# First MLP of a decoder trunk: down products with the features on the partitions, summed in place on the residual

## Chip, core and metric

The kernel runs on one NeuronCore of a Trainium2 chip. The metric is device time in microseconds (us) from the first to the last instruction of the program, with what the device does around it; the median of several executions is given. In what follows PE is TensorE (matrix products, into PSUM), ScalarE is ACT in the profile, VectorE is DVE, GpSimd is POOL, and SP is the engine whose queue issues most DMAs.

## What is computed

The reference is a trunk of two layers over 512 tokens with 1024 features, all in float32:

```
for i in range(2):
    x = x + mixer_i(rms_norm(x, norm_mix[i]))        # 0: latent attention, 1: gated linear attention
    x = x + square(relu(rms_norm(x, norm_mlp[i]) @ w_up[i])) @ w_down[i]   # 1024 -> 4096 -> 1024
return rms_norm(x, final_norm)
```

This case is about the first of the two MLPs, that of layer 0. Behind it comes the norm of layer 1's gated linear attention, which wants its input with the features on the partitions. Behind the second MLP comes the final norm and the output, which is written with the tokens on the partitions.

## The kernel before

**Products in three parts.** Each float32 operand is split into a high part, rounded to the fast float32 format (`fp32r`), and the low rest. A product is high.high + high.low + low.high: three matmuls into one PSUM bank. `split` (lines 110 and 113) makes the two parts, the high one on ScalarE, the low one on VectorE; `piece` does it for a block of weights and puts the parts in the rooms `wh` and `wl`, four of each. A room has 1152 elements a partition and holds 1024; `at` says at which element the weights begin: `W_AT` is 128, `AT_UP` is 124 for the high and 60 for the low part. The normed input of the MLP lies at an offset of its own (`X_AT`, 44), and the tile `T` with its quadrant combinations begins at element 4 of its room. Hidden activations and their parts lie in "slots" (`slot("B")`), 512 elements each, from the slot's start; four pairs of slots are the rooms of the hidden parts (`parts_room`), used in turn.

**The MLP in blocks and quadrants.** The hidden width of 4096 is worked off in eight blocks of 512. The first block's up product is done plainly (`up_first`), the last block's down product too, at the end; the seven steps between do the down product of one block and the up product of the next. Each of the two is cut into quadrants (token halves, halves of the feature and hidden range) and done with seven quadrant products in place of eight, after the scheme of Strassen and Winograd, with sums and differences of quadrants on VectorE and in the weight loads (GpSimd's DMAs that add). `step` is the order of the first of the seven steps, in which up and down products alternate; `step_in_halves` is that of the other six, first the up products, then the down products. `quadrants()` makes the combinations of the input.

**Up and down products.** `up_product` (matmuls at line 962) has the weights as the stationary operand and the input as the moving one: output with hidden features on the partitions, 24 matmuls of 128x256. `down_product` (matmuls at line 971) has the hidden parts as the stationary operand and the weights as the moving one: output with the tokens on the partitions, two token tiles of 512 features each, 12 matmuls of 128x512. A PSUM tile of two banks (`d`, `e`) or two single banks (`u`) takes it.

**The sums.** The seven down products of a step are added up in five sums of 128x1024: S11, S12, S21, SU and S5. Four lie in the room of the residual `xall` (its eight tiles `xT[0..7]` have the features on the partitions), S5 in a tile of its own. A sum is carried on either by copying it into PSUM first, letting the product add to it and copying it back (`onto`, ScalarE), or by a VectorE addition. In the second MLP (`nxt` is None) `residual()` turns the residual into token-major form on PE (line 910), so that the sums start from it. In the first MLP (`nxt` is the next norm) the sums start from nothing (`opening` in `step`): the first copies overwrite `xall`, and the residual is saved before in DRAM as `x_kept` by a DMA on SP's queue (line 1166, after the load of d12) and loaded again at the end, in four pieces, into the `comb` tiles of four weight quadrants that are no longer used (`before_next`, line 1184, `kept`).

**The end of the first MLP.** Per output feature tile (`p`, eight of them in two groups of four): four transposes on PE turn the sums' 128x128 pieces into the PSUM bank (line 1233), 12 matmuls of 128x512 add the last block's plain down product (line 1240), VectorE adds the kept residual and writes `xT[m]` (line 1242), and `nxt.add` scales, splits and squares it for the next norm (lines 262, 263, 248 to 252). The hidden parts of the last block lie in the four rooms of `parts_room`. The next norm's mean comes from a product at line 277.

**What sets the order.** Every engine runs its own instructions in the order the program has them for that engine; the framework that builds the kernel places instructions by a plan of its own with costs, so that it may put a later line ahead of an earlier one where the data allow it. DMAs are issued on SP's and GpSimd's queues in order. Waits between engines are semaphores.

Of the kernel before, what the change touches and what calls it, by code (L numbers as in the profile page):

```python
# [50 lines left out]
def trunk_kernel(ctx: ExitStack, tc: tile.TileContext, t_in: dict, out: bass.AP):  # L51
# [763 lines left out]
    def mlp(layer, nrm, nxt=None):  # L815
# [7 lines left out]
        if nxt:  # L823
            dram = es.enter_context(tc.tile_pool(name=f"spill{layer}", bufs=1, space=bass.MemoryType.DRAM))
            x_kept = dram.tile([P, ND, S], F32, name="x_kept")

# [3 lines left out]
        sums = [xall[:, 2 * i : 2 * i + 2].rearrange("p a t -> p (a t)") for i in range(4)]  # L830
        sums.append(fast.tile([P, 2 * S], F32, tag="sum", name="sum5"))
        S11, S12, SU, S21, S5 = sums
# [70 lines left out]
        def residual():  # L903
            def turned(tag, c, th):
# [59 lines left out]
        def down_product(t, a, parts, start):  # L964
            wh, wl = piece(a, 2, 512)
# [8 lines left out]
        def step(b, q, r, after):  # L974
            opening = nxt is not None
# [7 lines left out]
            def add(total, t):  # L983
                if opening:
                    ACT.activation(total, t, AF.Copy)
                else:
                    DVE.tensor_tensor(total, t, total, ALU.add)

            def onto(tag, total, a, parts, fresh=False):
                t = two_banks(tag)  # L990
                if not fresh:
                    ACT.activation(t, total, AF.Copy)
                down_product(t, a, parts, fresh)
                ACT.activation(total, t, AF.Copy)
# [12 lines left out]
            if opening:  # L1007
                ACT.activation(S11, d, AF.Copy)
            e = two_banks("e") if opening else begun(d)
# [5 lines left out]
            down_product(e, d12, parts_of_quad(q21), opening)  # L1015
            DVE.tensor_tensor(S11, e, S11, ALU.add)
# [58 lines left out]
            def down_21():  # L1075
                onto("d", S21, d22, parts_of_quad(q21, -1.0), opening)
                after("d22")
# [9 lines left out]
        def step_in_halves(b, q, r, after):  # L1087
# [9 lines left out]
            def onto(total, a, parts):  # L1097
                pair = [bank("u"), bank("u")]
                cols = [total[:, i * 512 : (i + 1) * 512] for i in range(2)]
                for p, c in zip(pair, cols):  # L1100
                    copied(p, c)
                down_product(pair, a, parts, False)
                for p, c in zip(pair, cols):
                    copied(c, p)
# [38 lines left out]
            DVE.tensor_tensor(S11, e, S11, ALU.add)  # L1143
# [9 lines left out]
            DVE.tensor_tensor(S12, e, S12, ALU.add)  # L1153
            after("d12")
            down_product(d, ds3, parts_of_quad(q12), False)
            DVE.tensor_tensor(SU, d, SU, ALU.add)
# [4 lines left out]
        if not nxt:  # L1161
            residual()
        for name in ("S1", "dS1", "d11", "A1", "d12", "dS3", "A2", "d22"):
            if name == "dS3" and nxt:
                with tc.issue_after(queued.ins):
                    SP.dma_start(x_kept, xall)
            queued = fetch(0, name)
        last_raw, last, gain, kept = [], [[], []], [], []
# [12 lines left out]
        def before_next(name):  # L1181
            if name in ("d11", "S1", "d12", "dS3"):
                t = by_k(comb(home[name]), 2)
                SP.dma_start(t, x_kept[:, 2 * len(kept) : 2 * len(kept) + 2])
                kept.append(t)
# [30 lines left out]
        if nxt:  # L1216
            room = [parts_room[(turn[0] + k) % 4] for k in range(4)]
# [5 lines left out]
            for c in range(2):  # L1223
# [5 lines left out]
                for j, p in enumerate(ps_):  # L1229
                    for t in range(NT):  # L1230
                        o = t % 2 * 512 + j * P
                        src = (S11, S12, S21, SU)[2 * c + t // 2][:, o : o + P]
                        PE.matmul(p[:, t * P : (t + 1) * P], src, ident, start=t == 0, stop=False, is_transpose=True, skip_group_check=True)
                for j, p in enumerate(ps_):
                    if j % 2 == 0:
                        w = piece(last_raw[c][:, :, j * P : (j + 2) * P], 4, 256)
                    for k in range(4):
                        wh, wl = cut(w, slice(None), k, slice(j % 2 * P, (j % 2 + 1) * P))
                        for n, (a, x) in enumerate(((wh, room[k][0]), (wh, room[k][1]), (wl, room[k][0]))):
                            PE.matmul(p, a, x, start=False, stop=k == 3 and n == 2, skip_group_check=True)  # L1240
                    m = 4 * c + j
                    DVE.tensor_tensor(xT[m], p, kept[m // 2][:, m % 2], ALU.add)
# [615 lines left out]
```

## Time and profile before

| | |
|---|---|
| median of 3 executions | 1046.12 us (1045.90 to 1046.43) |
| profiled execution, span from its first to its last instruction | 1044.9 us |
| PE busy | 1035.0 us, 99% |
| weight loads of PE busy | 903.9 us, 87% |
| VectorE busy | 876.9 us, 84% |
| ScalarE busy | 696.8 us, 67% |
| first MLP, first up product of the steps to the last down product | 206.79 to 474.67 us |
| its last products | to 500.13 us |
| second MLP, residual transposes to the last down product | 743.23 to 1014.64 us |
| read from HBM, written | 144.49 MB, 4.19 MB |

How to read it: the profiled execution's own time is the span; the timed executions, which have no profiler, lie some 1.2 us above it. "Busy" of PE includes the latency of the last matmul of each run, so 99% doesn't mean that every cycle does work; the rate of a run of matmuls is read from the pieces of the chain of waits, which give the start of a piece, its length, and how many instructions it has. In a row of the groups view stand the line, engine, operation, output and inputs, shape, count, then the busy time and the mean duration of one; behind the second bar the idle time of the engine just before and who ended it. In a row of the timeline stand start, length, engine, line; idle time before the instruction and its releaser stand in brackets.

### The profile page before, as it was taken

What the parts mean: (1) busy time and instruction counts of PE and PEld (TensorE: products, weight loads), DVE (VectorE), ACT (ScalarE), POOL (GpSimd) and SP (SyncE); (2) the same over time, 40 slices, a digit from 0 to 9 for tenths busy, and PEclk for the clock granted to TensorE, in tenths of its full rate; (3) what the DMA queues carried; (4) which work ended last, traced back from release to release, by engine and by line L of the source; (5) the groups of instructions that cost most, each with busy time, mean ns of one, the idle gap of its engine ahead of it and who ended that gap; (6) DMA issues with size and microseconds to landing.
All of it is one profiled execution on the core that took longest, in us unless ns stands there. A gap on an engine that the chain in (4) does not pass through costs nothing.

```text
span 1044.9 us, 15747 instructions
## 1 busy us (share of the span) xinstructions
PE 1035.0 (99%) x5966; PEld 903.9 (87%) x5966; DVE 876.9 (84%) x1340; ACT 696.8 (67%) x1122; POOL 114.3 (11%) x128
## 2 busy tenths in 40 slices
PE   9999999999999999999999999999999999999997
PEld 8788888899899899898888888888889989989986
DVE  7889977988989989989687399469798999898993
ACT  8667754577776776785445566555677677677784
POOL 8400010301101101000000000000011111110000
PEclk9999999999999999999999999999999999999999
DMA  7401235769878778644212222165488778778422
GB/s 232 122 21 41 81 95 147 224 166 215 216 191 202 178 203 202 161 136 126 77 55 82 87 74 75 48 162 147 95 241 201 185 202 198 194 191 191 111 81 81
DMA packets 120717, 149.98 MB, mean 144 GB/s; under 512 B 9568, under 2 KB 86368, under 8 KB 120512
## 3 DMA queue, kind: packets, MB, share of 16 engines
q1 hardware_dynamic: 96144, 117.76, 35.4%
q0 software_dynamic: 22400, 29.36, 18.0%
q10 hardware_dynamic: 2096, 1.84, 0.6%
q8 instruction: 47, 0.77, 0.3%
q14 instruction: 30, 0.25, 0.1%
HBM read 144.49 MB, written 4.19 MB: 142 GB/s over the span
## 4 chain that ended last, share of the span: by engine, by line
PE 94%; DVE 3%; ACT 2%; issue 0%; DMA 0%; ACTq 0%; SPq 0%; DVEq 0%
PE ps L971 25%; PE ps L962 25%; PE ps L118 10%; PE ps L120 10%; PE ps L119 10%; PE ps L1279 2%; PE ps L1240 2%; PE ps L1499 1%; PE ps L135 1%; PE ps L421 1%; PE ps L1626 1%; DVE wl L113 1%; PE ps L1766 0%; PE ps L1549 0%; PE ps L684 0%
## 5 line engine op out<-in xcount | busy, mean ns | idle before, releaser
L971 PE MATMUL ps<-wh,set 128*128 128x512 f32 x784 | 245.7, 390 | 0.3 <-ACT set L110 0.3
L110 ACT ACTIVATE wh<-wraw 128x1024 fp32r<-128x1024 f32 x139 | 146.4, 1056 | 110.2 <-PE ps L119 42.6
L113 DVE TENSOR_TENSOR wl<-wraw,wh 128x1024 fp32r<-128x1024 f32 x139 | 169.7, 1222 | 39.0 <-ACT wh L110 38.7
L971 PEld LDWEIGHTS ps<-wh,set 128*128 128x128 f32 x784 | 147.0, 188 | 30.7 <-ACT set L110 0.7
L962 PE MATMUL ps<-T,wh 128*128 128x256 f32 x896 | 154.9, 275 | 0.0
L971 PE MATMUL ps<-wl,set 128*128 128x512 f32 x392 | 152.6, 389 | 0.0
L113 DVE TENSOR_TENSOR wl<-comb,wh 128x1024 fp32r<-128x1024 f32 x112 | 136.8, 1221 | 18.5 <-ACT wh L110 18.3
L110 ACT ACTIVATE wh<-comb 128x1024 fp32r<-128x1024 f32 x112 | 118.3, 1057 | 47.6 <-issue 28.7
L962 PEld LDWEIGHTS ps<-T,wh 128*128 128x128 f32 x896 | 135.4, 188 | 0.4
L962 PE MATMUL ps<-T,wl 128*128 128x256 f32 x448 | 123.4, 275 | 0.0
L962 PE MATMUL ps<-set,wh 128*128 128x256 f32 x672 | 117.1, 276 | 0.0
L118 PE MATMUL ps<-set,wh 128*128 128x512 f32 x280 | 109.7, 392 | 0.0
L119 PE MATMUL ps<-set,wh 128*128 128x512 f32 x280 | 109.6, 392 | 0.0
L120 PE MATMUL ps<-set,wl 128*128 128x512 f32 x280 | 109.3, 391 | 0.0
L962 PEld LDWEIGHTS ps<-set,wh 128*128 128x128 f32 x672 | 102.6, 188 | 1.3
L962 PE MATMUL ps<-set,wl 128*128 128x256 f32 x336 | 92.7, 276 | 0.0
L971 PEld LDWEIGHTS ps<-wl,set 128*128 128x128 f32 x392 | 73.6, 188 | 14.7
L962 PEld LDWEIGHTS ps<-T,wl 128*128 128x128 f32 x448 | 84.1, 188 | 0.1
L962 PEld LDWEIGHTS ps<-set,wl 128*128 128x128 f32 x336 | 63.1, 188 | 0.0
L120 PEld LDWEIGHTS ps<-set,wl 128*128 128x128 f32 x280 | 52.6, 188 | 11.1
L119 PEld LDWEIGHTS ps<-set,wh 128*128 128x128 f32 x280 | 52.6, 188 | 11.1 <-DVE set L750 0.2
L118 PEld LDWEIGHTS ps<-set,wh 128*128 128x128 f32 x280 | 52.6, 188 | 10.7
(415 smaller groups left out, 2015.4 us busy)
## 6 DMA issues: line engine op xcount, KB each, us to landing
comb<-in_mlp_w_down_dram SPq DMA_DIRECT2D x74, 512.0 KB, 4.1
wraw<-in_mlp_w_up_dram SPq DMA_DIRECT2D x18, 1024.0 KB, 5.6
comb<-in_mlp_w_down_dram POOLq DMA_DIRECT2D x28, 512.0 KB, 6.5
wraw<-in_mlp_w_up_dram SPq DMA_DIRECT2D x28, 512.0 KB, 5.6
wraw<-in_gla_w_in_dram SPq DMA_DIRECT2D x12, 1024.0 KB, 5.2
comb<-in_mlp_w_up_dram SPq DMA_DIRECT2D x14, 512.0 KB, 4.4
comb<-in_mlp_w_up_dram POOLq DMA_DIRECT2D x14, 512.0 KB, 6.4
wraw<-in_mlp_w_up_dram POOLq DMA_DIRECT2D x14, 512.0 KB, 7.6
```

What stands on the lines that cost most here:

```text
L110: order(ACT.activation(hi, src, AF.Copy))
L113: lo_eng.tensor_tensor(lo, src, f(hi), ALU.subtract)
L118: PE.matmul(psum, wh, xh, start=start, stop=False)
L119: PE.matmul(psum, wh, xl, start=False, stop=False)
L120: PE.matmul(psum, wl, xh, start=False, stop=stop)
L135: PE.transpose(psum, src, ident[: src.shape[0], : src.shape[0]])
L421: PE.matmul(p, w[:, i, j * P : (j + 1) * P], x, start=start, stop=stop)
L962: PE.matmul(o, a_, x_, start=start and j == 0 and k == 0 and n == 0, stop=k == KH - 1 and n == 2, skip_group_check=True)
L971: PE.matmul(o, x_, w_, start=start and k == 0 and n == 0, stop=k == 1 and n == 2, skip_group_check=True)
L1240: PE.matmul(p, a, x, start=False, stop=k == 3 and n == 2, skip_group_check=True)
L1279: PE.matmul(o, a, b_, start=False, stop=k == 3 and n == 2, skip_group_check=True)
L1499: PE.matmul(p[:, t - t0], k[:, t * P : (t + 1) * P], moving[:, t], start=True, stop=True)
```

## The change

All of it is in the first MLP; the second one keeps its form. Five things:

1. `down_product` takes the weights as the stationary operand and the hidden parts as the moving one: four feature tiles of 128x256, 24 matmuls. The weights' parts are put at `AT_UP` in their rooms.
2. The sums S11, S12, S21 and SU are the quadrants of the residual itself: feature half by token half of `xall`, as strided views of 4 x 256. `laid` gives PSUM tiles the same form. `residual()` does for the first MLP what the scheme needs of start values: SU is negated, and S21 becomes -S21 - SU.
3. `opening` is gone: the first step adds to its sums as the second MLP's does (`begun`, `add` on VectorE, `onto` with a copy first).
4. `x_kept`, its DMA to DRAM and the four loads of `kept` are gone.
5. At the end there are no transposes: the first matmul of each final product opens its bank, and VectorE adds `xT[m]` in place. The last of the four rooms of hidden parts is no longer the oldest of `parts_room` but a `comb` tile, the one that S1's weights had.

```diff
-            x_kept = dram.tile([P, ND, S], F32, name="x_kept")
...
+        if nxt:
+            S11, S12, S21, SU = (xall[:, c * KH : (c + 1) * KH, t] for c in range(2) for t in (first, second))
+        else:
+            S11, S12, SU, S21 = (xall[:, 2 * i : 2 * i + 2].rearrange("p a t -> p (a t)") for i in range(4))
...
         def residual():
+            if nxt:
+                ACT.activation(SU, SU, AF.Copy, scale=-1.0)
+                DVE.scalar_tensor_tensor(S21, S21, -1.0, SU, ALU.mult, ALU.subtract)
+                return
...
         def down_product(t, a, parts, start):
-            wh, wl = piece(a, 2, 512)
+            wh, wl = piece(a, 2, 512, at=AT_UP if nxt else (W_AT, W_AT))
+            if nxt:
+                for j in range(4):
+                    o = t[j // 2][:, j % 2 * TH : (j % 2 + 1) * TH] if isinstance(t, list) else t[:, j * TH : (j + 1) * TH]
+                    for k in range(2):
+                        xh, xl = cut(parts, slice(None), slice(k * TH, (k + 1) * TH))
+                        a_h, a_l = (w_[:, k, j * P : (j + 1) * P] for w_ in (wh, wl))
+                        for n, (w_, x_) in enumerate(((a_h, xh), (a_h, xl), (a_l, xh))):
+                            PE.matmul(o, w_, x_, start=start and j % 2 == 0 and k == 0 and n == 0, stop=k == 1 and n == 2, skip_group_check=True)
+                return
...
-            if opening:
-                ACT.activation(S11, d, AF.Copy)
-            e = two_banks("e") if opening else begun(d)
+            e = begun(d)
...
-                onto("d", S21, d22, parts_of_quad(q21, -1.0), opening)
+                onto("d", S21, d22, parts_of_quad(q21, -1.0))
...
-            if name == "dS3" and nxt:
-                with tc.issue_after(queued.ins):
-                    SP.dma_start(x_kept, xall)
...
-            if name in ("d11", "S1", "d12", "dS3"):
-                t = by_k(comb(home[name]), 2)
-                SP.dma_start(t, x_kept[:, 2 * len(kept) : 2 * len(kept) + 2])
-                kept.append(t)
...
-            room = [parts_room[(turn[0] + k) % 4] for k in range(4)]
+            spare = fast.tile([P, 2 * S], F32R, tag=f"comb{home['S1']}", bufs=1, name=uname("comb"))
+            room = [parts_room[(turn[0] + k) % 4] for k in range(3)] + [(spare[:, :S], spare[:, S:])]
...
-                    for t in range(NT):
-                        o = t % 2 * 512 + j * P
-                        src = (S11, S12, S21, SU)[2 * c + t // 2][:, o : o + P]
-                        PE.matmul(p[:, t * P : (t + 1) * P], src, ident, start=t == 0, stop=False, is_transpose=True, skip_group_check=True)
-                for j, p in enumerate(ps_):
...
-                            PE.matmul(p, a, x, start=False, stop=k == 3 and n == 2, skip_group_check=True)
+                            PE.matmul(p, a, x, start=k == 0 and n == 0, stop=k == 3 and n == 2)
                     m = 4 * c + j
-                    DVE.tensor_tensor(xT[m], p, kept[m // 2][:, m % 2], ALU.add)
+                    DVE.tensor_tensor(xT[m], p, xT[m], ALU.add)
```

44 lines of the change are left out of this document (20 added, 24 removed).

## The prediction

> **What bounds the kernel now.** I read the page first, then the chain of waits around the first MLP, then the engines' busy time in that stretch.
>
> ```profile
> span 1044.9 us, 15747 instructions
> ...
> PE 1035.0 (99%) x5966; PEld 903.9 (87%) x5966; DVE 876.9 (84%) x1340; ACT 696.8 (67%) x1122; POOL 114.3 (11%) x128
> ...
> PE 94%; DVE 3%; ACT 2%; issue 0%; DMA 0%; ACTq 0%; SPq 0%; DVEq 0%
> PE ps L971 25%; PE ps L962 25%; PE ps L118 10%; PE ps L120 10%; PE ps L119 10%; PE ps L1279 2%; PE ps L1240 2%; PE ps L1499 1%; PE ps L135 1%; PE ps L421 1%; PE ps L1626 1%; DVE wl L113 1%; PE ps L1766 0%; PE ps L1549 0%; PE ps L684 0%
> ```
>
> TensorE (PE) is the bound: 94% of the chain that ended last is its matmuls, half of that the up products (L962) and down products (L971). So what the change does to the time is read from PE's stream. The two MLPs, each from its first product (or residual transpose) to its last down product, stand in the windows view; the columns after the stretch are its length and each engine's busy us, then granted clock, DMA share and GB/s.
>
> ```profile
> 206.79:474.67 267.88, 267.73 (x1765) 244.17 (x1764) 240.84 (x266) 200.00 (x278) 31.93 (x27) 1.00 0.74 183
> 743.23:1014.64 271.41, 271.23 (x1796) 247.58 (x1795) 245.04 (x270) 202.64 (x280) 29.88 (x24) 1.00 0.70 174
> ```
>
> In the first MLP's 267.88 us PE idles 0.15 us, at the full clock. VectorE (240.84 us) and ScalarE (200.00 us) have room, DMA too. A saving on PE is therefore a saving in time, and every nanosecond added per matmul is a loss: nothing covers it.
>
> **The transposes removed.** Pieces of the chain of waits at the end of the first MLP (start, length, what):
>
> ```profile
> 474.83 1.75 PE ps L1233 x16
> 476.58 10.91 PE ps L1240 x48
> 487.49 1.75 PE ps L1233 x16
> 489.23 10.90 PE ps L1240 x48
> ```
>
> The 32 transposes that turn the token-major sums stand on the chain with nothing idle before or behind them, 2 x 1.75 = 3.50 us. Gone from PE: -3.50 us. The 96 products behind them stay, now opened by their own first matmul.
>
> **The down products.** A product was 12 matmuls of 512 columns (hidden parts stationary, weights moving); it becomes 24 of 256 (weights stationary, hidden parts moving). The window of the first MLP has 392 + 196 = 588 of the old ones, so 49 products, and 1176 matmuls after.
>
> ```profile
> L971 PE MATMUL ps<-wh,set 128*128 128x512 f32 x392 | 122.9, 390 | 0.2 <-ACT set L110 0.2
> ...
> L971 PE MATMUL ps<-wl,set 128*128 128x512 f32 x196 | 76.3, 389 | 0.0
> ```
>
> The 390 ns is latency, pipelined; the rate is in the chain:
>
> ```profile
> 206.95 2.74 PE ps L962 x24
> ...
> 766.84 2.75 PE ps L971 x12
> ...
> 588.45 1.42 PE ps L1626 x12
> ...
> 596.39 2.48 PE ps L1626 x21
> ```
>
> An up product, already 24 matmuls of 256 columns with weights stationary, takes 2.74 us; a down product of 12 by 512 takes 2.75. At the up product's rate (114 ns a matmul) the new form costs the same: 49 x (2.74 - 2.75) = -0.5 us, which is rounding; I take 0. But the third and fourth rows are matmuls of the same 128x256 shape in the linear-attention stage, and they come at 1.42/12 = 118 ns and 2.48/21 = 118 ns. With those, a product is 24 x 118.2 = 2.84 us: 49 x 0.09 = +4.4 to +4.8 us. What differs between the two is the place of the operands in SBUF: the up product's weights lie at elements 124 and 60 of their rooms (`AT_UP`) and its moving operands at 44 or 4 (`X_AT`, the `T` tile), whereas those of L1626 begin where their tiles begin. The new down product has the weights at `AT_UP` and the moving parts at the start of their slots: half of the up product's placing. These are the two ends, 0 and +4.8. I take the lower: weights by code, shape, order (wh.xh, wh.xl, wl.xh) and the two-halves-per-bank output are the up product's, and its rate holds for L962's two kinds of moving tile alike (T and the normed input), far apart in SBUF. It is the step I am least sure of.
>
> The Trainium skill (TensorE: Matmul & The Clock Gate, Back-to-back issue gap) gives each warm matmul a fixed cost of about 2.5 ns beside its columns; by that, 588 more matmuls would cost an estimated 1.5 us, and the sum would be 1.5 us higher. The trace disagrees: 24 matmuls of 256 and 12 of 512 take the same within 0.01 us. The skill (SBUF — State Buffer, SBUF: two separate sides) also holds that TensorE's reads wait for nobody, which would make the placing indifferent and the lower end certain; the 118 ns rows do not fit that, so it does not decide here.
>
> **Start of the first MLP.** `residual()` now runs in it: one ScalarE negation and one VectorE combination of 128x1024, no transposes. The copies of the first sums go from L1008 (to SBUF) to `begun` (to PSUM), as the second MLP has them.
>
> ```profile
> 212.79 1.01 ACT L1008 ACTIVATE xT<-ps 128x1024 f32<-128x1024 f32 x1
> 213.69 1.05 ACT L110 ACTIVATE wh<-comb 128x1024 fp32r<-128x1024 f32 x1
> ...
> 752.98 1.01 ACT L980 ACTIVATE ps<-ps 128x1024 f32<-128x1024 f32 x1
> ...
> 748.93 1.23 DVE L918 SCALAR_TENSOR_TENSOR xT<-ps,xT 128x1024 f32<-128x1024 f32 x1 [1.08 <-ACT xT L917]
> ...
> 229.79 1.01 ACT L985 ACTIVATE xT<-ps 128x1024 f32<-128x1024 f32 x1
> ...
> 769.63 1.23 DVE L987 TENSOR_TENSOR xT<-ps,xT 128x1024 f32<-128x1024 f32 x1 [0.56 <-PE ps L971]
> ...
> 214.78 1.23 DVE L113 TENSOR_TENSOR wl<-comb,wh 128x1024 fp32r<-128x1024 f32 x1 [1.17 <-ACT wh L110]
> ...
> 217.84 0.50 PE L971 MATMUL ps<-wh,set 128*128 128x512 f32 x1 [0.15 <-ACT set L110]
> ```
>
> The same copy costs 1.01 us in both. The negation adds about 1.05 us on ScalarE, the combination 1.23 us on VectorE. Also new: the two `add`s move from ScalarE (L985, 1.01) to VectorE (as L987, 1.23), and one copy before the d22 product (1.01). The d12 product, and all PE work queued behind it, now waits for `begun`'s copy of d; that copy would end at 213.8, the product stands at 217.84, with the 24 up matmuls (2.74 us) and more between. All of it lies beside PE: the second MLP runs that very step with three copies and one combination more. Its stretch, less the same 3.50 us for its own 32 transposes, is 271.41 - 3.50 = 267.9, the first MLP's 267.88: the ScalarE and VectorE work of an in-place residual costs nothing. If cover fails, it is VectorE's 1.23 us ahead of the first step: VectorE idles 1.17 us before 214.78, so at most some 0.1 us reaches the one place where PE waits (0.15 us at 217.84); if that idle time were gone, 1.2 us. I take 0 (bounds -0.15 and +1.2).
>
> **DRAM copies removed.** One write and four reads leave SP's queue.
>
> ```profile
> L1184 SPq DMA_DIRECT2D comb<-x_kept x4: 320/338/338, 434.5 to 467.4; - x4
> L1166 SPq DMA_DIRECT2D x_kept<-xT x1: 470/470/470, 192.7 to 192.7; - x1
> ```
>
> Behind them stand weight loads, which come sooner; PE waits for none of these now, so 0. No bound below that: the whole PE idle is 0.15 us.
>
> **Hand-over to the next layer.** PE arrives 1.75 us earlier at the last products. Rows of ScalarE and VectorE there:
>
> ```profile
> 474.63 0.42 ACT L110 ACTIVATE set<-set 128x256 fp32r<-128x256 f32 x1 [0.26 <-PE ps L971]
> ...
> 476.23 0.42 DVE L113 TENSOR_TENSOR set<-set,set 128x256 fp32r<-128x256 f32 x1
> ...
> 479.96 0.69 DVE L1242 TENSOR_TENSOR xT<-ps,comb 128x512 f32<-128x512 f32 x1
> ...
> 486.88 0.75 DVE L263 SCALAR_TENSOR_TENSOR set<-xT,gains,set 128x512 fp32r<-128x512 f32 x1 [0.79 <-ACT set L262]
> ...
> 492.01 0.69 DVE L1242 TENSOR_TENSOR xT<-ps,comb 128x512 f32<-128x512 f32 x1 [0.78 <-PE ps L1240]
> 493.49 0.75 DVE L263 SCALAR_TENSOR_TENSOR set<-xT,gains,set 128x512 fp32r<-128x512 f32 x1 [0.79 <-ACT set L262]
> ...
> 499.53 0.75 DVE L263 SCALAR_TENSOR_TENSOR set<-xT,gains,set 128x512 fp32r<-128x512 f32 x1 [0.79 <-ACT set L262]
> ...
> 504.58 0.69 DVE L113 TENSOR_TENSOR tmp<-acc,tmp 128x512 fp32r<-128x512 f32 x1 [0.70 <-ACT tmp L110]
> ...
> 506.93 0.45 PE ps L277 x2
> ```
>
> The last hidden part is ready at 476.65; PE would start at 474.83 and needs it in the fourth k-block, 10 matmuls (10.91/48 each) or 2.3 us later, at 477.1. That split waited for the last down product (474.63) because it reused that product's room; the change gives it a free one, so it comes sooner. VectorE then has to run 3.5 us earlier too. Its idle time up to 500 is 0.79 + 0.78 + 0.79 + 0.79 = 3.15 us, and the norm's sum is ready at 504.58 + 0.69 = 505.27, 1.66 us before PE uses it at 506.93. So 3.15 + 1.66 = 4.8 us of slack for 3.5: 0, and if none of the idle time can be filled, 3.5 - 1.66 = +1.8. The one cost I do count: the fourth room is a `comb` tile, off the slots' placing, for 3 of each 12 final products, 24 matmuls of 227 ns; at the 4% of the 118 ns rows, +0.2 us.
>
> **Sum.** -3.50 + 0 + 0 + 0 + 0.2 = -3.3 us. On the profiled execution, 1044.9 becomes 1041.6; the median of the runs lies 1.2 us above that span (launch and end, unchanged): 1046.1 - 3.3 = **1042.8 us**. Its own range, with the small bounds, is 1042.0 to 1044.0.
>
> **Rivals.**
> *Placing costs (other side).* The 1176 new matmuls run at L1626's 118 ns. For it: moving slots start at the same kind of place there, and only placed operands show 114. Against: weights are placed, and runs of 12 and 21 are short. It decides from 3.3 us / 1176 = 2.8 ns above the old rate, at about 117 ns. At 118.2: +4.8 - 3.3 = +1.5, so 1047.6; two ns more and it is 1050.
> *Hand-over gives it back.* VectorE, not PE, paces the last eight tiles, and PE waits at L277: +1.8 at most, 1044.6. For it: VectorE runs without a break from 473 to 486. Against: the slack above.
> *Each matmul has a fixed cost.* The rounding of 2.74 and 2.75 leaves up to 0.02 us a product, 49 x 0.02 = +1.0: 1043.8. The skill's rule above would put it at 1044.3.
> *No change at all*, the transposes having been cover for something: PE's records show no wait behind them that they hide, save the 1.8 us just costed.
>
> **How the numbers follow.** Forecast 0.46; placing 0.33; hand-over 0.12; fixed cost 0.05; nothing 0.04. What a measurement of this kernel can tell from no change is about 0.2%, 2.1 us: below 1044.0 is faster, above 1048.2 slower. Faster: all of the forecast and the better part of the fixed cost, 0.49. Slower: the placing above 118.8 ns, somewhat under half of its 0.33, and a little for an order of instructions that turns out worse, 0.18. Within: the rest, 0.33. The range takes in the forecast's lower end and the placing to 119.3 ns: **1041.8 to 1048.8**.
>
> **What would show it.** Rows to compare with (min/median/max of the latency in ns; bytes):
>
> ```profile
> L1626 PE MATMUL ps<-set,ADh x32: 277/280/282, 588.3 to 673.6; 128*128 128x256 f32 x32
> ...
> L962 PE MATMUL ps<-T,wh x896: 275/275/281, 215.0 to 995.6; 128*128 128x256 f32 x180
> ...
> HBM read 144.49 MB, written 4.19 MB: 142 GB/s over the span
> ```
>
>  Right: no L1233-like transposes between the last down product and the final ones, up to 3.5 us off the stretch from the first up product to the next layer; pieces of 24 down matmuls in 2.74 us; latency of 275 ns for them as in L962; PE idle in the first MLP still under 1 us; written bytes halved, 4.19 to 2.10 MB. Wrong: 24 in 2.82 or more, with latencies of 279 ns and up, as L1626 has; or idle time of PE ahead of the final products or at L277 with VectorE as releaser.

## The result, and the profile after

The changed kernel takes 1051.66 us (median of 4 runs, 1051.43 to 1052.22) against 1046.16 us of the kernel before (4 runs, 1045.90 to 1046.43): a ratio of 1.0056, with an interval of 1.0043 to 1.0068. It is slower, and the time lies outside the predicted range, on its upper side.

The page of the kernel after: span, busy time of the engines, DRAM traffic, and the shares of the chain that ended last, by engine and by line.

```profile
span 1049.9 us, 16847 instructions
...
PE 1039.6 (99%) x6522; PEld 930.1 (89%) x6522; DVE 881.2 (84%) x1343; ACT 697.7 (66%) x1122; POOL 113.9 (11%) x128
...
HBM read 142.39 MB, written 2.10 MB: 138 GB/s over the span
...
PE 91%; ACT 4%; DVE 4%; issue 1%; DMA 0%; ACTq 0%; SPq 0%; DVEq 0%
```

The copies in DRAM are gone (4.19 to 2.10 MB written, 2.10 MB less read). PE has 4.6 us more to do. Its share of the chain falls from 94% to 91%, but that share is not the loss: `place_order` below, which is faster than both, has 89%, since the chain leaves PE for ScalarE and VectorE in long stretches in which PE works all the same, here from 459.29 to 475.23 us. What was lost is read from the stretches and the pieces below.

The same stretches as before in the windows view of the kernel after: steps of the first MLP, its final products, and the second MLP (columns as in the prediction).

```profile
206.89:483.76 276.87, 275.56 (x2353) 274.12 (x2353) 245.41 (x271) 199.85 (x278) 30.98 (x26) 1.00 0.69 171
483.76:505.70 21.94, 21.94 (x96) 17.84 (x96) 20.53 (x27) 12.43 (x18) 0.00 (x0) 1.00 0.37 119
748.90:1020.46 271.56, 271.38 (x1797) 247.61 (x1796) 245.75 (x271) 203.43 (x281) 29.89 (x24) 1.00 0.69 174
```

And of the kernel before, cut at the same places (each of its two stretches holds 16 of the transposes):

```profile
206.79:476.58 269.79, 269.64 (x1782) 246.08 (x1781) 242.75 (x270) 201.33 (x279) 31.93 (x27) 1.00 0.74 184
476.58:500.13 23.55, 23.55 (x114) 19.73 (x113) 20.20 (x27) 11.85 (x18) 0.00 (x0) 1.00 0.35 112
```

All of the loss is in the steps: less their 1.75 us of transposes, they took 268.04 us and now take 276.87. PE is idle there for 1.31 us (276.87 - 275.56) in place of 0.15; the rest is slower work at a full clock (1.00). The second MLP, whose code is the same, is the same.

Of these 8.8 us a single step shows both parts. Pieces of the chain of waits of the kernel after (start, length, what), one step's up products (L973), its down products (L984) in two pieces, and the final products (L1242):

```profile
246.69 19.07 PE ps L973 x168
265.76 11.53 PE ps L984 x96
277.28 0.04 DVEq L113
277.32 0.31 DVE set L851
277.63 0.04 issue
277.67 8.48 PE ps L984 x70
...
483.76 22.11 PE ps L1242 x96
```

The same seven down products before:

```profile
264.95 19.07 PE ps L971 x84
```

84 matmuls of 512 columns took 19.07 us, 227 ns each. Now 96 of 256 columns take 11.53 us, **120.1 ns** each, where the up products' 168 of the same shape take 19.07, 113.5 ns each. And behind these PE **waits** about 0.4 us (0.04 + 0.31 + 0.04) for L851 of VectorE, once a step: at 277.3, 316.7, 356.2, 395.7, 435.3 and 474.7.

Where the stretch from the first up product to the last final product went, from PE's records of each trace (the time from the start of each matmul to the start of the next, summed over lines; the last three columns are experiments, below):

| us | before | after | `place` | `order` | `place_order` |
|---|---|---|---|---|---|
| up products of the steps (1176) | 134.0 | 134.0 | 133.9 | 133.9 | 133.9 |
| down products (588, then 1176) | 133.8 | 142.9 | 140.6 | 141.1 | 133.9 |
| transposes | 3.3 | 0 | 0 | 0 | 0 |
| final products (96) | 22.0 | 22.1 | 22.1 | 22.1 | 22.1 |
| sum | 293.2 | 299.0 | 296.6 | 297.2 | 289.9 |

The down products' +9.1 us are 6.3 of rate and 2.8 of waits. Without the matmuls at a wait the mean is 119.1 ns, against 113.8 for half of an old one: 1176 x 5.3 ns. At each of the six waits two intervals are long, 441 to 553 ns, and then 223 to 225 ns, since PE's next weight load too had stood still: (2782 + 1348 - 12 x 119) ns = 2.7 us; one more interval of 223 ns in the first step makes it 2.8. The transposes' 3.3 become 3.5 with the first product behind each group of them, which took 314 ns in place of 227. The sum is +5.8; the span has +5.0, because of a wait at the end of the second MLP that is shorter here (last section).

### The profile page after: what moved, and what is told of

Its sections match the earlier page's. It is cut to its first block, busy times and chain, and to the rows that moved or that the text cites. A ratio compares the mean times of both kernels' runs of the same rounds, so it can differ in the third digit from the quotient of the medians.

```text
span 1049.9 us, 16847 instructions
## 1 busy us (share of the span) xinstructions
PE 1039.6 (99%) x6522; PEld 930.1 (89%) x6522; DVE 881.2 (84%) x1343; ACT 697.7 (66%) x1122; POOL 113.9 (11%) x128
## 4 chain that ended last, share of the span: by engine, by line
PE 91%; ACT 4%; DVE 4%; issue 1%; DMA 0%; ACTq 0%; SPq 0%; DVEq 0%
PE ps L973 24%; PE ps L984 12%; PE ps L991 11%; PE ps L118 10%; PE ps L120 10%; PE ps L119 10%; PE ps L1281 2%; PE ps L1242 2%; PE ps L1501 1%; PE ps L135 1%; PE ps L421 1%; DVE wl L113 1%; ACT wh L110 1%; PE ps L1628 1%; DVE set L113 1%
## 5 line engine op out<-in xcount | busy, mean ns | idle before, releaser
L113 DVE TENSOR_TENSOR wl<-wraw,wh 128x1024 fp32r<-128x1024 f32 x139 | 169.7, 1222 | 41.2 <-ACT wh L110 41.0
L973 PE MATMUL ps<-T,wh 128*128 128x256 f32 x896 | 154.8, 275 | 0.0
L110 ACT ACTIVATE wh<-comb 128x1024 fp32r<-128x1024 f32 x112 | 118.7, 1060 | 54.1 <-issue 28.7
L113 DVE TENSOR_TENSOR wl<-comb,wh 128x1024 fp32r<-128x1024 f32 x112 | 136.8, 1222 | 16.2 <-ACT wh L110 15.6
L984 PE MATMUL ps<-set,wh 128*128 128x256 f32 x784 | 142.5, 281 | 1.3 <-DVE set L851 1.1
L973 PEld LDWEIGHTS ps<-T,wh 128*128 128x128 f32 x896 | 135.2, 188 | 0.2
L973 PE MATMUL ps<-T,wl 128*128 128x256 f32 x448 | 123.3, 275 | 0.0
L984 PEld LDWEIGHTS ps<-set,wh 128*128 128x128 f32 x784 | 120.6, 188 | 2.8 <-DVE set L851 2.3
L991 PE MATMUL ps<-wh,set 128*128 128x512 f32 x392 | 122.9, 390 | 0.2 <-ACT set L110 0.2
L973 PE MATMUL ps<-set,wh 128*128 128x256 f32 x672 | 117.0, 276 | 0.0
L984 PE MATMUL ps<-set,wl 128*128 128x256 f32 x392 | 109.6, 280 | 0.0
L973 PEld LDWEIGHTS ps<-set,wh 128*128 128x128 f32 x672 | 102.0, 188 | 0.7
L973 PE MATMUL ps<-set,wl 128*128 128x256 f32 x336 | 92.7, 276 | 0.0
L991 PEld LDWEIGHTS ps<-wh,set 128*128 128x128 f32 x392 | 73.5, 188 | 15.4 <-ACT set L110 0.4
L973 PEld LDWEIGHTS ps<-T,wl 128*128 128x128 f32 x448 | 84.1, 188 | 0.0
L991 PE MATMUL ps<-wl,set 128*128 128x512 f32 x196 | 76.3, 389 | 0.0
L984 PEld LDWEIGHTS ps<-set,wl 128*128 128x128 f32 x392 | 73.5, 188 | 0.0
L973 PEld LDWEIGHTS ps<-set,wl 128*128 128x128 f32 x336 | 63.1, 188 | 0.0
```

Source lines behind the costliest of these rows:

```text
L110: order(ACT.activation(hi, src, AF.Copy))
L113: lo_eng.tensor_tensor(lo, src, f(hi), ALU.subtract)
L973: PE.matmul(o, a_, x_, start=start and j == 0 and k == 0 and n == 0, stop=k == KH - 1 and n == 2, skip_group_check=True)
L984: PE.matmul(o, w_, x_, start=start and j % 2 == 0 and k == 0 and n == 0, stop=k == 1 and n == 2, skip_group_check=True)
L991: PE.matmul(o, x_, w_, start=start and k == 0 and n == 0, stop=k == 1 and n == 2, skip_group_check=True)
```

## Experiments

Two things were in question: why a matmul of 256 columns takes 120 ns in one place and 113 in another, and what the wait is. All kernels below are edits of the kernel after, but for `before_moved`. Times are medians; ratios are against the kernel before, timed on the same chip.

### Several places of the weights in one kernel: `sweep1`, `sweep2`

Each of the seven steps gets a place of its own for the parts of the down product's weights; `sweep2` also exchanges the second and third matmul of a product, so that the low part of the moving operand comes last.

```diff
+        calls, PLACES = [0], ((124, 60), (128, 128), (80, 16), (16, 80), (128, 64), (64, 128), (124, 60))
...
-            wh, wl = piece(a, 2, 512, at=AT_UP if nxt else (W_AT, W_AT))
+            at = PLACES[calls[0] // 7] if nxt else (W_AT, W_AT)
+            calls[0] += 1
+            wh, wl = piece(a, 2, 512, at=at)
...
-                        for n, (w_, x_) in enumerate(((a_h, xh), (a_h, xl), (a_l, xh))):       # sweep2 alone
+                        for n, (w_, x_) in enumerate(((a_h, xh), (a_l, xh), (a_h, xl))):
```

> The changed kernel, but each of the seven steps puts the down weights at another place in their rooms (element of the high and of the low part): step 0 124/60, 1 128/128, 2 80/16, 3 16/80, 4 128/64, 5 64/128, 6 124/60 again. Steps 0 and 6 serve as the control. Theory A, placing: the 256-column down matmuls come at about 120 ns in steps 0 and 6, and at another rate in at least one of the others; 80/16 stands to the moving parts as the up product's weights stand to theirs (64 elements and 16 apart), so if only the distance counts, step 2 has 113 to 114 ns. Theory B, form: the rate belongs to the 128x256 form with the hidden parts as moving operand, whatever the weights' place: all steps 117 to 122 ns, and the median of single down matmuls does not move by more than 1 ns between steps.

> As sweep1, with the three matmuls of a product in the order high.high, low.high, high.low, so that the low part of the hidden activations is needed by the third matmul and not by the second. Theory C, late low part: the one gap of some 0.33 us between the first and the second matmul of the last or next to last down product of each step (six of 0.44 to 0.55 us between starts in the changed kernel) shrinks to under 0.25 us or is gone. Its rival: the wait is VectorE's queue being late altogether, then the gap only moves to the third matmul, with the same 0.3 us. For the rate, theory A expects that order and place act together, so that the fastest place may be another than in sweep1; theory B again 117 to 122 ns everywhere.

Measured: 1052.18 and 1048.87 us (a single execution each). The chain of `sweep1` (L987 is its down product, L974 the up product), from the third step's down products at 305.63 to the next ones, and the fifth step's:

```profile
305.63 10.90 PE ps L987 x96
...
316.57 0.18 DVE wl L113
316.75 0.61 DVE set L852
...
317.40 8.20 PE ps L987 x70
...
383.71 11.53 PE ps L987 x96
395.27 0.30 DVE set L852
...
395.62 8.66 PE ps L987 x70
```

At (80, 16) 96 matmuls take 10.90 us, 113.5 ns each; at (128, 64) they take 11.53. The chain of `sweep2` at steps 2 and 3 of the places' list (counted from 1: (128, 128), then (80, 16)), each 168 down products in one piece:

```profile
266.15 20.15 PE ps L987 x168
...
305.37 19.05 PE ps L987 x168
```

So the place of the weights alone, in the same kernel, with the same kind of moving operands and at a full clock (1.00), sets the rate: 20.15 / 168 = 119.9 ns or 19.05 / 168 = 113.4 ns. And (16, 80) is as good as (80, 16): which part lies where doesn't matter. What (80, 16) has in common with the up product is a distance. By the addresses that the compiled program gives its tiles, slots and weight rooms all begin at byte 32 modulo 256, so the weights begin 4 x 80 = 320 or 4 x 16 = 64 bytes behind the moving operand, both 64 modulo 256. In the up product the weights begin at byte 16 and the moving operand, `T` or the normed input, at 208, modulo 256: again a **distance of 64**. With `AT_UP` and a slot it is 240.

The wait answers to the edit of the order: `sweep2` has no such gap in any step; by which way is told below (What the wait is). In `sweep1` the gap grows where the products are faster (0.87 us from 316.53 to 317.40 against 0.38 from 395.24 to 395.62), since PE arrives sooner.

### The moving side: `moving`

If it is the distance, moving the other operand must do as well. Two of the four pairs of parts get rooms in the unused token half of the normed input's tiles, where they begin as the normed input does; weights stay at `AT_UP`. Their down products then have a distance of 64, the other two pairs' products still 240. (The final products keep to slots and the `comb` room.)

```diff
+            def lent(r):
+                o = X_AT + r * 4 * S
+                v = both_room[0][:, o : o + 4 * S].rearrange("p (k a t) -> p k a t", k=2, a=2)
+                return v[:, :, 0, second], v[:, :, 1, second]
...
+            parts_room = [lent(0), own[0], lent(1), own[1]]
```

> The changed kernel, but two of the four rooms of hidden parts lie in the token half of the normed input's lead tiles that no product reads after the first block, that is at the offset of the up product's moving operands; the weights stay at 124/60. Rooms are taken in turn, so every second down product is of the new kind. Theory A: products with the lent rooms come at 113 to 114 ns a matmul (2.72 to 2.74 us for 24), those with slots at 117 to 122 ns; if all seven steps behave so, the first MLP is some 24 x 24 x 6 ns = 3.5 us shorter. Theory B: no difference between the two kinds, 117 to 122 ns.

Measured: 1049.80 us (a single execution). In its chain the first step's third, fourth and fifth down products, in a lent room, a slot, and a lent room:

```profile
220.85 2.74 PE ps L998 x24
...
226.31 2.87 PE ps L998 x24
...
234.65 2.72 PE ps L998 x24
```

2.72 / 24 = 113.3 ns from the lent room, 2.87 / 24 = 119.6 ns from the slot, by turns. Neither the weights' place nor the moving operand's is good or bad by itself. The stretch of the table above is 296.7 us, 2.3 less than after and not the 3.5 that were expected: five of the six waits are left, and since PE comes sooner they have grown (long intervals of 623 to 740 ns).

### Each cause alone, and both: `order`, `place`, `place_order`

```diff
-            wh, wl = piece(a, 2, 512, at=AT_UP if nxt else (W_AT, W_AT))
+            wh, wl = piece(a, 2, 512, at=(80, 16) if nxt else (W_AT, W_AT))                 # place, place_order
...
-                        for n, (w_, x_) in enumerate(((a_h, xh), (a_h, xl), (a_l, xh))):
+                        for n, (w_, x_) in enumerate(((a_h, xh), (a_l, xh), (a_h, xl))):       # order, place_order
```

> The changed kernel with the order high.high, low.high, high.low in the down products alone, weights at 124/60. Theory C: six gaps of some 0.33 us go, -1.5 to -2.3 us against the changed kernel, so 1049.4 to 1050.2 us; the rate may change by a ns a matmul either way (1.2 us). If VectorE is late altogether: no gain, 1051.4 to 1051.9.

> The changed kernel with one edit: the down weights at elements 80 and 16 of their rooms in place of 124 and 60, in all seven steps. Theory A (distance of the operands' starts): 1176 matmuls fall from 119.9 to 113.4 ns, -7.6 us; but the low part of the hidden activations is then still later against PE (sweep1 had that gap at 0.93 us between starts in the well-placed steps, 0.44 in the others), some +0.5 us in six steps: 1046.5 to 1048 us. If the rate gained nothing on the path: 1051 to 1052.

> Both edits: weights at 80/16 and the order high.high, low.high, high.low. If the two causes are all that the prediction missed, the time is the order's run (1050.4) less 7.6 us: 1042.5 to 1043.2 us, the -3.3 us that were forecast from the 32 transposes. If there is a third cost, it lies above 1044.

| | median us | ratio to before (interval) |
|---|---|---|
| after | 1051.66 | 1.0056 (1.0043 to 1.0068) |
| `order` | 1050.43 | 1.0043 (1.0027 to 1.0060) |
| `place` | 1048.98 | 1.0024 (1.0013 to 1.0036) |
| `place_order` | 1042.82 | 0.9971 (0.9960 to 0.9983) |

The chain of `order` for the step that was shown above:

```profile
265.72 20.15 PE ps L984 x168
```

of `place`:

```profile
264.92 10.90 PE ps L984 x96
...
275.86 0.19 DVE wl L113
276.05 0.61 DVE set L851
...
276.70 8.51 PE ps L984 x70
```

and of `place_order`, with its last down products and the final ones:

```profile
264.81 19.05 PE ps L984 x168
...
455.34 19.40 PE ps L984 x168
474.75 22.08 PE ps L1242 x96
```

Against the kernel after, the two edits don't add up: -1.2 and -2.7 us alone, -8.8 together. `order` takes the waits away and nothing of the rate (20.15 for 168); it gains 1.8 us in the stretch by the table above, less than the 2.7 of the waits, since all its steps now run at 120.0 ns, where the kernel after came out of each wait at some 118 and so had a mean of 119.1. `place` mends the rate, but PE then comes sooner to a low part that VectorE delivers hardly any sooner (at 276.65 us, 11.7 behind the step's first down product, where it was 11.9): the first long interval grows from 441-553 to 930-1175 ns, and the six waits cost (5847 + 1345 - 12 x 114) ns = 5.8 us in all, 3.1 more than in the kernel after. With both, every step's down products take what the old form took, 19.05 us, and the kernel is faster than before.

What the wait is, in the timeline of the kernel after: PE and, below, VectorE.

```profile
277.11 0.40 PE L984 MATMUL ps<-set,wh 128*128 128x256 f32 x2
277.67 0.39 PE L984 MATMUL ps<-set,wh 128*128 128x256 f32 x1 [0.17 <-DVE set L851]
```

```profile
274.67 1.22 DVE L1157 TENSOR_TENSOR xT<-ps,xT 128x1024 f32<-128x1024 f32 x1
275.80 1.22 DVE L113 TENSOR_TENSOR wl<-comb,wh 128x1024 fp32r<-128x1024 f32 x1
276.93 0.69 DVE L851 SCALAR_TENSOR_TENSOR set<-set,set 128x512 fp32r<-128x512 f32 x1
```

The product's first matmuls, high by high, run (x2); the next wants the low part of the hidden activations, at about 277.34 (118 ns behind the start of the second). L851 finishes it at 277.62, behind an addition (L1157) and a weight split (L113) on VectorE without a break. In the kernel before, the same three instructions on VectorE:

```profile
273.65 1.22 DVE L1143 TENSOR_TENSOR xT<-ps,xT 128x1024 f32<-128x1024 f32 x1
274.78 0.68 DVE L845 SCALAR_TENSOR_TENSOR set<-set,set 128x512 fp32r<-128x512 f32 x1
275.38 1.22 DVE L113 TENSOR_TENSOR wl<-comb,wh 128x1024 fp32r<-128x1024 f32 x1
```

There the low part (L845) comes **ahead of the weight split** and ends at 275.46; the third matmul of its product takes it at 276.15, so it had 0.7 us to spare. In the new order of three it is wanted sooner, by some 0.2 to 0.3 us, which alone would not have used that up. What makes the wait is that the framework's plan now has the split of 1.22 us first. It is so in all six steps of the kernel after, of `place` and of `sweep1`; in `order`, `sweep2`, `sweep3` and `place_order` the low part is ahead of the split in all six, and PE doesn't wait for it (in `order` it ends at 276.45 and is taken at 277.31). Had VectorE kept the old order, L851 would have ended in the kernel after at an estimated 275.80 + 0.68 = 276.48, 0.9 us ahead of need. `moving` has both: five steps with the split first, which wait, and the last one with the low part first:

```profile
472.03 0.68 DVE L863 SCALAR_TENSOR_TENSOR set<-set,set 128x512 fp32r<-128x512 f32 x1
472.62 1.22 DVE L113 TENSOR_TENSOR wl<-comb,wh 128x1024 fp32r<-128x1024 f32 x1
```

There the low part is still wanted by the second matmul, and the interval ahead of it is 196 ns, some 80 above the rate, where the long ones of the other five steps are 623 to 740. So the edit of the matmuls' order mends the wait mainly through VectorE's order, and not by asking for the part one matmul later. No run changes VectorE's order alone, and why the plan turns with the order of three matmuls on another engine stays open.

### Only the weights moved, old form: `before_moved`

The kernel before, with the down products' weights (moving there) at `AT_UP`, in both MLPs:

```diff
-            wh, wl = piece(a, 2, 512)
+            wh, wl = piece(a, 2, 512, at=AT_UP)
```

> The kernel before, with one edit: the down weights of both MLPs, there the moving operand of 128x512 matmuls, at 124/60 in place of 128/128. Theory A says that the distance counts for this form too: its 1176 matmuls go from 227 ns to 230 to 236, so 1049 to 1056 us. If placing matters only where weight loads and matmuls take about the same time (256 columns), the rate stays at 226 to 228 ns and the time at 1045 to 1047 us.

Measured: 1051.85 us (a single execution), 6.0 us slower than the kernel before on the same chip (median 1045.80). Its chain, the seven down products of the same step:

```profile
264.88 19.59 PE ps L971 x84
```

19.59 / 84 = 233.2 ns, against 227.0 with weights and parts at equal starts. So the effect isn't one of the new form or of 256 columns. Here, though, the good distance is 0 and the bad one is 16 modulo 256, while at 256 columns 0 is bad (119.9 ns, step 2 of `sweep2`).

### More distances: `sweep3`

`place_order` with these places in steps 1 to 7; the distances modulo 256 are 64, 128, 192, 32, 48, 80 and 96 bytes.

```diff
+        calls, PLACES = [0], ((16, 16), (32, 96), (48, 112), (8, 72), (12, 76), (20, 84), (24, 88))
```

> place_order, but with the down weights at other places in each step; the start of the weights less the start of the moving parts, in bytes modulo 256, is: step 0 64 (both parts at element 16), 1 128 (32/96), 2 192 (48/112), 3 32 (8/72), 4 48 (12/76), 5 80 (20/84), 6 96 (24/88). Known so far: 64 gives 113.4 ns, 0 and 240 give 119.9. If 64 alone locks, step 0 has 113 to 114 ns and the others 117 to 121. If every distance from 64 to 192 is far enough, steps 1, 2, 5 and 6 have 113 to 114 too.

Measured: 1047.30 us (a single execution). Its chain, the first step's third down product (64) and all of steps 2, 4, 6 and 7 (128, 32, 80, 96):

```profile
226.66 2.73 PE ps L987 x24
...
264.82 19.94 PE ps L987 x168
...
342.70 19.88 PE ps L987 x168
...
420.52 20.16 PE ps L987 x168
...
459.73 19.71 PE ps L987 x168
```

In ns for a matmul of 128x256: 113.6 at 64; 118.7, 118.4, 120.0 and 117.3 at 128, 32, 80 and 96; 117.8 at 48 and at 192. Among these distances it is one narrow place, not a slope: 16 bytes off it, a third of the gain is left at 48 and none at 80. Each distance but 64, 0 and 240 was measured in one step of one kernel.

### The transposes put back: `turns`

`place_order` with the 32 transposes ahead of the final products, as before; their results aren't used.

```diff
+                    for t in range(NT):
+                        src = xT[4 * c + j][:, t * P : (t + 1) * P]
+                        PE.matmul(p[:, t * P : (t + 1) * P], src, ident, start=t == 0, stop=t == NT - 1, is_transpose=True, skip_group_check=True)
```

> place_order with 32 transposes of 128x128 put back ahead of the final products, four for each output tile, of the sums, into the bank that the first product matmul then opens anew (so they compute nothing that is used). If the transposes were wholly on the path, as the prediction's -3.50 us holds: 1042.8 + 3.5 = 1046.3 us. If they covered something (weights or hidden parts late at the hand-over), less than 3.5 us come back: 1043 to 1045.5.

Measured: 1046.80 us, ratio 1.0008 (0.9999 to 1.0018), 4.0 us above `place_order`. Its chain:

```profile
475.07 1.75 PE ps L1239 x16
476.82 11.05 PE ps L1246 x48
487.86 1.75 PE ps L1239 x16
```

The stretch from first up product to last final product is 293.4 us, `place_order`'s 289.9: the transposes cost their 3.5 us, nothing beside them hid them, and nothing behind them was waiting for another engine. The rest of the 4.0 us is a wait at the end of the second MLP (last section).

### Two loose ends: `place_order_spare`, `place_order_x`

The room of the last hidden parts as a pair of slots in place of a `comb` tile; and the plain up products' weights, at a distance of 0 from the normed input, moved to 64 (all else as `place_order`).

```diff
-            spare = fast.tile([P, 2 * S], F32R, tag=f"comb{home['S1']}", bufs=1, name=uname("comb"))
-            room = [parts_room[(turn[0] + k) % 4] for k in range(3)] + [(spare[:, :S], spare[:, S:])]
+            spare = slot("B"), slot("B")                                                       # place_order_spare
+            room = [parts_room[(turn[0] + k) % 4] for k in range(3)] + [spare]
...
-    AT_X, AT_UP = (X_AT, X_AT), (124, 60)
+    AT_X, AT_UP = (124, 60), (124, 60)                                                         # place_order_x
```

> As place_order, with the last room of hidden parts for the final products in two slots that are free by then, in place of the comb tile. The 24 matmuls that read it come at 227 and not 233 ns, and the three to six behind each recover at once: 0.2 to 0.4 us less than place_order, if the slots' wait (the parts of the last down products must have been read) stays hidden. Otherwise the same or up to 0.5 us more.

> place_order, with the weights of the plain up products (matmuls of 128x512 with the normed input moving, 96 at the start of each MLP and 96 in the pairs) at 124/60 in place of 44/44: distance 64 from the moving operand modulo 256, as the up products have it. They now alternate between 228 and 232 ns. If the distance that serves 256 columns serves 512 as well: 227 ns, 0.5 to 1.0 us less than place_order, 1042.0 to 1042.5. If 512 columns want equal starts (as the down products of the kernel before have, 227 ns at distance 0): 230 to 236 ns, the same or up to 0.7 us more.

`place_order_spare`: 1042.82 us, ratio 0.9970 (0.9958 to 0.9982). Its chain at the final products:

```profile
474.86 21.78 PE ps L1242 x96
```

21.78 us against 22.08, so the `comb` room cost 0.3 us there. Another 0.3 us went in the down products of the last step, 19.10 in place of 19.40 us; the median is the same, and neither is seen in it.

`place_order_x`: 1042.34 us, ratio 0.9963 (0.9949 to 0.9977). It is the fastest of all and beats both kernels; 0.5 us below `place_order`, with runs that overlap (1041.51 to 1042.62 and 1042.32 to 1043.18). In its trace a matmul of the plain up products takes 227.5 ns from start to start, in `place_order`'s 231.0. With 512 columns a distance of 64 is here as good as 0 is in the down products of the kernel before, while 0 between the normed input and its weights isn't.

## Why the prediction was wrong, step by step

**The bound.** Right: PE set the time, and each nanosecond a matmul was a loss. 1176 x 5.3 ns are most of the loss.

**The transposes.** Right, -3.50: `turns` brings back 3.5 us in the trace.

**The down products: the step that failed.** The term was taken as 0 out of 0 to +4.8. It measured +9.1: 6.3 of rate, 2.8 of waits. The lower end was chosen because "weights by code, shape, order (wh.xh, wh.xl, wl.xh) and the two-halves-per-bank output are the up product's". The kernel after has all of these at 119.1 ns, and `place`, which changes nothing but the weights' place, runs at 113.5 up to each wait (10.90 / 96). The rows quoted there already held the answer: L962 at 114 ns against L1626 at 118, one shape. The working even named the difference, the place of operands, and then asked whether *half* of the good placing is good enough. By the runs at 256 columns the place of one operand by itself means nothing; the distance between the two starts does, and half of a placing is a new distance, 240 here. L1626's operands lie at 32 and 192, and take 118.2 and 117.9 ns; `sweep3` shows 118.4 and 117.8 at these two (L1626's runs are short, and a short run can be at 118 for another reason, see the last section). "Its rate holds for L962's two kinds of moving tile alike" proved nothing: both begin at byte 208 modulo 256.

Latencies are as foreseen under "wrong", 279 ns in the median; with the distance mended they are 276, close to the up product's 275 (rows of L984, min/median/max, of the kernel after, then of `place_order`):

```profile
L984 PE MATMUL ps<-set,wh x784: 276/279/387, 209.5 to 483.4; 128*128 128x256 f32 x196
```

```profile
L984 PE MATMUL ps<-set,wh x784: 276/276/385, 209.5 to 474.5; 128*128 128x256 f32 x196
```

**The wait that was costed at nothing.** PE's idle time in the steps was to stay under 1 us and came to 1.31, and the waits cost 2.8 us in all. The prediction took VectorE's instructions in the order that they had; an order "that turns out worse" stands in it only as a little of a chance. The plan did turn: the low part of the hidden activations, which had 0.7 us to spare, now stands behind a weight split of 1.22 us. The order of the three matmuls was given there as a reason for a rate, and not asked as a question of time: when is each part wanted, and what stands ahead of it on the engine that makes it?

**The rival "placing costs".** It held in its mechanism, and it was the right one of the other side; its price was too low, 118 in place of 120 ns, because it took the nearest rows' distance for this one's. "Two ns more and it is 1050" is what came, with the wait on top: 1051.7. Its point of decision, 117 ns, holds: at 113.4 ns the kernel gains 3.0 us (`place_order`), at 120.0 without the wait (`order`) it loses 4.6. Its thresholds of 118.8 and 119.3 ns leave out the 0.2 us of the `comb` room; with it they are 118.6 and 119.1.

**Fixed cost per matmul.** Refuted: 168 of 256 columns take 19.05 us and 84 of 512 19.07. By the formula of the Trainium skill (TensorE: Matmul & The Clock Gate, Back-to-back issue gap) for the gap of a single warm matmul, with its 2.5 ns beside the columns, the 84 more would cost an estimated 0.2 us a step; `place_order` shows none of it.

**Start of the first MLP, DRAM copies, hand-over.** Right, 0 each. In `place_order`, which has all three, the stretch is 3.3 us shorter than before, which is the transposes' 3.5 less 0.2 of all the rest together; the rooms of the final products cost 0.1 to 0.3 of the 0.2 that was counted. Bytes written were halved as foretold. The rival of the hand-over has no support: L277's products begin 6.80 us behind the last of the final ones before, 6.81 after and 6.82 in `place_order` (506.93, 512.68 and 503.65 us).

**The sum.** -3.3 and 1042.8 us were the time of a kernel with the distance right and the low part last: `place_order` measured 1042.82 us. That the two agree to 0.02 us is chance: against the kernel before on the same chip it gains 3.0 us, and the stretch is 3.3 us shorter. That all other terms held isn't an excuse for the one taken at its lower end: a term with ends 4.8 us apart, in a sum of 3.3, was the whole question.

## What to carry to other kernels

When a product is turned round, or an operand gets another room, work out the distance between the starts of stationary and moving operand (here modulo 256 bytes), and compare it with that of the fastest matmuls of that shape in the same trace; read rates from long pieces of the chain (count by length), where 6 ns of 114 are plain. When the matmuls of a product are cut or ordered otherwise, compare the order of the instructions on the engine that makes their operands too, before and after: the framework may have turned it, and the part that is made last is safest in the last matmul. And where two causes hide each other, as a slow rate hides a late operand, mending one alone may show little.

## What the runs showed of the hardware that was not expected

**A matmul's rate depends on how its two operands lie to each other in SBUF.** For 128x256 in `fp32r`, in long runs, by the distance of starts modulo 256 bytes (stationary less moving): 113.4 ns at 64; 119.9 at 0, 117.8 at 48, 118.4 at 32, 120.0 at 80, 117.3 at 96, 118.7 at 128, 117.8 at 192, 119.9 at 240. For 128x512: 227.0 to 227.5 at 0 with both at a slot's place and at 64, but 231 at 0 with both at byte 208, and 233 at 16. The final products that read the `comb` room stand at 64 too, with the moving operand at byte 224, and take 233 ns. So the distance isn't the whole rule for 512 columns. At 256 columns two pairs of starts have the distance of 64, moving at 32 (`place_order`) and at 208 (lent rooms of `moving`, up products), and both are fast; at the other distances of this list the moving operand began at 32. The mechanism isn't shown by any run here. The Trainium skill (SBUF — State Buffer, SBUF: two separate sides) says that TensorE never waits for another user of SBUF. In these runs, nonetheless, the start address alone, in one kernel and order, takes 168 matmuls from 19.05 to 20.15 us (`sweep2`).

**The rate has a memory.** At one distance, 64, the 70 matmuls behind a wait take 8.20 us in `sweep1` (317.40) and 8.51 in `place` (276.70): in four of `place`'s six waits the rest of the step runs at 117 to 119 ns, in the other two it is back at 113 to 114 after some six matmuls. The last step of `place_order` does the same behind one interval of 162 ns, 19.40 us in place of 19.05. So of the distances tried 64 alone gives 113.4 ns, and it isn't always enough where the stream has been interrupted; what decides it wasn't found.

**One wait moves by itself.** The second MLP's end, whose code is alike in all these kernels, has one wait of PE for ScalarE that changes from kernel to kernel. From the start of one matmul to the next it is 1.50 us before, 0.61 after, 0.59 in `place_order`, 1.16 in `place_order_spare` and 1.37 in `turns`. It hides or adds up to 0.9 us of what an edit far ahead of it does, which is why the span after is only 5.0 us longer and why what `place_order_spare` gains doesn't show. Its cause was not looked for and stays open.
